# Two heads of attention side by side, and each pair's value products between the projections of the next pair

## The chip, the cores and the metric

One core of one Trainium2 chip runs the program. The time is that of the device, in microseconds, for one execution.

## The reference, cut to what matters

The input `x` has 512 tokens of width 1024. A first block (a gated convolution with a linear recurrence, then a layer that picks experts per token) changes it. A second block mixes it again, and the change lies in that one. It projects the normalised tokens to 4096 columns. Half of them feed an attention with eight heads of width 64. The other half feed four heads of a gated delta rule, a recurrence over chunks of tokens. The two outputs are gated, joined, projected back to width 1024 and added to the input.

With 512 tokens the block selection of the attention picks nothing away, so it comes down to causal attention with a slope per head:

```
logit = q @ k.T / 8 - slope * (t - s)          (for s <= t)
p     = softmax(logit)
out   = (p @ v) * silu(z)
```

## The kernel before, in words

All data of the second block is held with features on the 128 partitions and the 512 tokens along them, in float32. The projections are exact products split in three: each weight and each activation is a high part and a low part, and a projection is 3 x 8 matmuls of 128 x 128 by 512 columns (`_mm3`, lines 108 to 112, in `proj`, lines 861 to 866). The products of the attention take plain float32, and the trace shows two matmuls for each of them.

A **pair** is two heads. A projection has 128 output rows, so that head 2j lies on partitions 0 to 63 and head 2j+1 on 64 to 127. `attention(j)` (lines 1082 to 1136) works on pair j:

- Lines 1083 to 1097: four projections, for queries `aq`, keys `ak`, values and the gate `az`. The values are turned to token order by four transposes, in a bank of tag "pa" (line 1092).
- Lines 1105 to 1121, for one head: four blocks of 128 queries. Each does a product of 128 queries with the 128 to 512 keys that they may see (line 1108, contraction over the head's 64 rows), adds the slope (VectorE, line 1111), takes the maximum (1114, 1115), the exponential with its sum (ScalarE, 1116) and divides (1118, 1119).
- Lines 1122 to 1134, for the same head: four blocks of 128 keys. Each is transposed on TensorE (1126), copied out of PSUM (VectorE for odd blocks at line 1129, ScalarE for even ones at 1131) and multiplied with the values (1132), into the head's 64 rows of one bank `po`.
- Then the other head does the same two loops. At last `po` is multiplied with the gate (1135).

In PSUM, "pp" has two banks for projections, "pa" two banks, "ps" three banks for the delta rule, and "po" one bank. The logits and the transposed probabilities of the attention share the two banks of "pa".

The order of the work is woven by hand and then arranged by a list scheduler. Every routine is a generator that yields after each step. `A` is the chain of the delta heads and their recurrence; `B` is two sets of delta inputs and then `attention(0)` to `attention(3)`. `weave(A, na, B, nb)` takes `na` steps of A and spreads `nb` steps of B among them:

```
PLAN = [(18, 8), (18, 60), (12, 24)]
...
    for na, nb in PLAN:
        weave(A, na, B, nb)
    for _ in A:
        pass
    G = chain(gates_of_delta(), gated_norm())
    weave(B, 200, G, 10)
```

A pair takes 21 steps, so that the 60 and 24 of the plan hold all four pairs. `G` projects the delta rule's gates (line 1143, four projections) and transposes and gates its output (1155, 1157); it comes after A and B. The tile framework then schedules all of it by a model of time: an instruction that is ready goes ahead of one that waits, so the order on each engine in the trace is not that of the code. Each engine runs its own list in order. The weights come on SyncE's queue in the order of `ORDER` and are split by ScalarE and VectorE (lines 103, 104).

After G, lines 1195 to 1198 split the four attention outputs, lines 1200 to 1202 those of the delta rule, and lines 1223 to 1232 project back; the attention's four chunks are the first half of that sum.

Lines 912 to 919, before the attention, turn the residual to token order and write it to memory by way of five buffers of tag "lg", which the attention uses afterwards for its logits.

Of the kernel before, what the change touches and what calls it, by code (L numbers as in the profile page):

```python
# [9 lines left out]
F32 = mybir.dt.float32  # L10
# [4 lines left out]
AF = mybir.ActivationFunctionType  # L15
OP = mybir.AluOpType
AX = mybir.AxisListType
# [3 lines left out]
P = 128  # L21
T = 512
# [90 lines left out]


OHB = 2
PLAN = [(18, 8), (18, 60), (12, 24)]
ORDER = [20, 16, 24, 21, 17, 25, 22, 18, 26, 23, 19, 27, 0, 4, 8, 12, 1, 5, 9, 13, 2, 6, 10, 14, 3, 7, 11, 15, 28, 29, 30, 31]


# [653 lines left out]
def _mixer2(k, psum, pv):  # L773

    nc, tc, I = k.nc, k.tc, k.I
    ctx, c4 = ExitStack(), ExitStack()
    p4 = c4.enter_context(tc.tile_pool(name="p4", bufs=1, reuse_waits="tile"))

    def tile_(name, tag, bufs, shape=(P, T), dt=F32):
        return p4.tile(list(shape), dt, name=name, tag=tag, bufs=bufs)  # L780
# [8 lines left out]
    for b in range(3):  # L789
        tok.append([])  # L790
        for h in range(2):
            o = tile_("ptok", *(("kT", 4), ("kT", 4), ("vT", 2))[b])
# [7 lines left out]
    C = {n: cb[:, slice(*v)] for n, v in _CB.items()}  # L800
# [6 lines left out]
    pps = ctx.enter_context(tc.tile_pool(name="ps4", bufs=1, space=PSUM, reuse_waits="tile"))  # L807
# [24 lines left out]
    for dc in range(KC):  # L832
        ps = bank("pt", "pa", (P, 4, P))
        for b in range(4):
# [3 lines left out]
                                       scalar=g2[:, dc:dc + 1], in1=x, op0=OP.mult, op1=OP.add)  # L838
        nc.scalar.activation(out=hH[:, dc, :], in_=x, func=AF.Copy, scale=fp[:, dc:dc + 1])
        nc.vector.scalar_tensor_tensor(out=hL[:, dc, :], in0=x, scalar=fp[:, dc:dc + 1],  # L840
                                       in1=hH[:, dc, :].bitcast(F32), op0=OP.mult, op1=OP.subtract)
# [27 lines left out]
    ps = bank("gates", "pa")  # L869
# [5 lines left out]
    ps = bank("gatesT", "ps", (P, 4, 8))  # L875
# [36 lines left out]
    for tb in range(4):  # L912
        for hf in range(2):
            ps = bank("x2", "pa", (P, 4, P))
            for j in range(4):
                nc.tensor.transpose(ps[:, j, :], xT[hf * 4 + j][:, tb * P:(tb + 1) * P], k.ident)
            o = tile_("x3", "lg", 5)
            nc.scalar.activation(out=o, in_=ps.rearrange("p a b -> p (a b)"), func=AF.Copy, scale=r1[:, tb:tb + 1])
            nc.sync.dma_start(out=k.x3d[tb, :, hf * T:(hf + 1) * T], in_=o)
    u_all = p4.tile([P, 4, 4, P], F32, name="u_all")  # L920
# [26 lines left out]
    def delta_inputs(h, ins):  # L947

        kT = qkv(20 + h, 4 + h, "kT", 4)
        yield  # L950
        q = qkv(16 + h, h, "qT", 4)
        yield
        vT = qkv(24 + h, 8 + h, "vT", 2)
        yield
        qT.append(q)
        sq = []
        for t in (kT, q):
            o = tile_("sq", "tmp", 3)
            nc.scalar.activation(out=o, in_=t, func=AF.Square)
            sq.append([o])  # L960
        rkq = p4.tile([P, 8], F32, name="rkq", tag="rkq", bufs=2)
        rstd(rkq, _token_sums(k, pps, sq, "ps", 3), 1.0)
        rk, rq = rkq[:, 0:4], rkq[:, 4:8]
        nc.vector.tensor_scalar(out=rq, in0=rq, scalar1=128.0 ** -0.5, scalar2=None, op0=OP.mult)
        sc = p4.tile([P, 3, 4], F32, name="ksc", tag="ksc", bufs=2)
        brk, bek, kdk = sc[:, 0, :], sc[:, 1, :], sc[:, 2, :]
        nc.vector.tensor_tensor(out=brk, in0=hcols(beta, h), in1=rk, op=OP.mult)
        nc.vector.tensor_tensor(out=bek, in0=brk, in1=hcols(egc, h), op=OP.mult)
        nc.vector.tensor_tensor(out=kdk, in0=hcols(kds, h), in1=rk, op=OP.mult)
        ins.append((h, kT, q, vT, rk, rq, brk, bek, kdk))  # L970
        yield
# [107 lines left out]
            S = S2  # L1079
            yield  # L1080

    def attention(j):
        aq, ak = tile_("aq", "aq", 2), tile_("ak", "ak", 2)
        nc.vector.scalar_tensor_tensor(out=aq, in0=proj(j), scalar=0.125, in1=row2, op0=OP.mult, op1=OP.mult)
        yield
        nc.vector.tensor_tensor(out=ak, in0=proj(4 + j), in1=row2, op=OP.mult)
        yield
        vT = tile_("vT", "tmp", 3)
        nc.vector.tensor_tensor(out=vT, in0=proj(8 + j), in1=row2, op=OP.mult)
        yield  # L1090
        av = tile_("av", "av", 2, (P, 4, P))
        nc.scalar.activation(out=av, in_=tokmajor(vT, "pa"), func=AF.Copy)
        yield
        az = tile_("az", "az", 4)
        nc.vector.tensor_tensor(out=az, in0=proj(12 + j), in1=row2, op=OP.mult)
        nc.scalar.activation(out=az, in_=az, func=AF.Silu)
        yield
        po = pps.tile([P, T], F32, name="ps_ao", tag="po", bufs=1)
        for hh in range(2):
            h = 2 * j + hh  # L1100
            off = hh * 64
            rows = slice(off, off + 64)
            slope = 2.0 ** -(h + 1)
            pr = []
            for qb in range(4):
                nk = (qb + 1) * P
                ps = pps.tile([P, T], F32, name="ps_l", tag="pa", bufs=2)
                nc.tensor.matmul(out=ps[:, 0:nk], lhsT=aq[rows, qb * P:(qb + 1) * P], rhs=ak[rows, 0:nk],
                                 start=True, stop=True)
                lg = tile_("lg", "lg", 5)  # L1110
                nc.vector.scalar_tensor_tensor(out=lg[:, 0:nk], in0=C["alibi"][:, 384 - qb * P:512], scalar=slope,
                                               in1=ps[:, 0:nk], op0=OP.mult, op1=OP.add)
                mx = p4.tile([P, 2], F32, name="mx", tag="mx", bufs=6)
                nc.vector.tensor_reduce(out=mx[:, 0:1], in_=lg[:, 0:nk], axis=AX.X, op=OP.max)
                nc.vector.tensor_scalar(out=mx[:, 0:1], in0=mx[:, 0:1], scalar1=-1.0, scalar2=None, op0=OP.mult)
                nc.scalar.activation(out=lg[:, 0:nk], in_=lg[:, 0:nk], func=AF.Exp, bias=mx[:, 0:1],
                                     accum_out=mx[:, 1:2])
                nc.vector.reciprocal(out=mx[:, 1:2], in_=mx[:, 1:2])
                nc.vector.tensor_scalar(out=lg[:, 0:nk], in0=lg[:, 0:nk], scalar1=mx[:, 1:2], scalar2=None, op0=OP.mult)
                pr.append(lg)  # L1120
                yield
            for kb in range(4):
                nq = (4 - kb) * P
                ps = pps.tile([P, T], F32, name="ps_pT", tag="pa", bufs=2)
                for qb in range(kb, 4):
                    nc.tensor.transpose(ps[:, (qb - kb) * P:(qb - kb + 1) * P], pr[qb][:, kb * P:(kb + 1) * P], k.ident)
                pT = tile_("pT", "pT", 3)
                if kb % 2:
                    nc.vector.tensor_copy(out=pT[:, 0:nq], in_=ps[:, 0:nq])
                else:  # L1130
                    nc.scalar.activation(out=pT[:, 0:nq], in_=ps[:, 0:nq], func=AF.Copy)
                nc.tensor.matmul(out=po[rows, kb * P:T], lhsT=av[:, kb, off:off + 64], rhs=pT[:, 0:nq],
                                 start=kb == 0, stop=kb == 3)
                yield
        nc.vector.tensor_tensor(out=az, in0=az, in1=po, op=OP.mult)
        azs.append(az)

    zs = []

    def gates_of_delta():  # L1140
        for h in range(4):
            z = tile_("dz", ("X", "XT")[h // 2], 2)
            nc.vector.tensor_tensor(out=z, in0=proj(28 + h), in1=row2, op=OP.mult)
            nc.scalar.activation(out=z, in_=z, func=AF.Silu)
            zs.append(z)
            yield
# [3 lines left out]
    def gated_norm():  # L1150

        for h in range(4):
            ps = bank("oT", "ps", (P, 4, P))
            for tb in range(4):
                nc.tensor.transpose(ps[:, tb, :], u_all[:, tb, h, :], k.ident)
            z = zs[h]
            nc.vector.scalar_tensor_tensor(out=z, in0=flat(ps), scalar=k.col("gdn_norm"), in1=z,
                                           op0=OP.mult, op1=OP.mult)
            yd.append(z)
            yield  # L1160

    def chain(*gens):
        for g in gens:
            yield from g
# [7 lines left out]
    def weave(a, na, b, nb):  # L1172

        done = 0
        for i in range(na):
            next(a, None)
            while (done + 1) * na <= (i + 1) * nb:
                next(b, None)
                done += 1

    ins = [[], []]
# [1 line left out]
        for _ in delta_inputs(h, ins[0]):  # L1183
            pass
    A = chain(heads(ins[0]), heads(ins[1]), recurrence())
    B = chain(delta_inputs(2, ins[1]), delta_inputs(3, ins[1]), *[attention(j) for j in range(4)])
    for na, nb in PLAN:
        weave(A, na, B, nb)
    for _ in A:
        pass  # L1190
    G = chain(gates_of_delta(), gated_norm())
    weave(B, 200, G, 10)
    for _ in G:
        pass
    for az in azs:
# [181 lines left out]
```

## Time and profile before

| | us |
|---|---|
| median of 3 runs | 1889.33 |
| lowest, highest | 1887.18, 1890.7 |
| the profiled execution | 1889.39 |
| its span | 1887.6 |
| TensorE busy in it | 1798.1 |
| attention, delta rule and recurrence | from about 1555 to 1833 of the span |

The span goes from the first to the last instruction that the profile holds; the profiled execution's own time is 1.79 us longer. In a timeline, a row's length is that of its group, and groups overlap; the time from one start to the next is what an instruction costs the engine. PE is TensorE's matmuls, PEld its weight loads, DVE VectorE, ACT ScalarE and SP SyncE. "x2" counts matmuls, of which a float32 product with values or keys has two.

### The profile page before, as it was taken

Reading aid. Unit: us, or ns where it says so; the run is one execution under the profiler, and the core shown is the slowest. Engines: PE = TensorE matmul, PEld = TensorE weight load, DVE = VectorE, ACT = ScalarE, POOL = GpSimd, SP = SyncE. Lnnn points to the kernel's source line nnn. Section 1 sums busy time; section 2 is a strip of 40 time slices with the busy share of each in tenths; the row PEclk is TensorE's granted clock in tenths of the full one; section 3 lists DMA queues with packets and bytes.
Section 4 is the critical chain, followed back from the end, with each engine's and each line's share of the span. In section 5 each row is a group of like instructions: output and inputs, shape, how many; then the busy total and the mean of one; then the engine's idle time right before and its main releaser. Section 6 shows DMA issues by size and latency. Waiting matters only on the chain.

```text
span 1887.6 us, 26152 instructions
## 1 busy us (share of the span) xinstructions
PE 1798.1 (95%) x9545; PEld 1541.1 (82%) x9545; DVE 1495.1 (79%) x3045; ACT 838.9 (44%) x1186; POOL 328.1 (17%) x260
## 2 busy tenths in 40 slices
PE   6979999999996999999999999999999999999988
PEld 4756678999985999999999999988887788767778
DVE  8995589999998988888878888889945774565665
ACT  4473343456883433333333333333334753454453
POOL 0000000000000035444444444445400000000000
PEclk9989899999997999999999999999999999999999
DMA  8951323335668979999999999999952321111022
GB/s 305 314 195 56 140 82 102 118 134 201 255 236 277 291 245 380 338 344 338 330 343 344 341 336 338 342 331 343 345 182 77 103 76 56 56 45 45 12 78 90
DMA packets 153412, 404.28 MB, mean 214 GB/s; under 512 B 12097, under 2 KB 64577, under 8 KB 151746
## 3 DMA queue, kind: packets, MB, share of 16 engines
q1 hardware_dynamic: 114690, 243.20, 37.6%
q0 software_dynamic: 36864, 134.23, 19.6%
q10 hardware_dynamic: 1728, 25.17, 3.4%
q8 instruction: 75, 1.23, 0.3%
q14 instruction: 55, 0.45, 0.1%
HBM read 370.05 MB, written 32.51 MB: 213 GB/s over the span
## 4 chain that ended last, share of the span: by engine, by line
PE 78%; DVE 10%; ACT 3%; issue 1%; DMA 1%; DVEq 0%; ACTq 0%; SPq 0%
PE pv L738 9%; PE pv L741 9%; PE pv L744 9%; PE psS L112 8%; PE psS L110 8%; PE psS L111 8%; PE ps_p L110 3%; PE ps_p L111 3%; PE ps_p L112 3%; PE ps_inv L930 2%; DVE wL L104 2%; PE ps_g L652 2%; PE ps_zp L110 1%; PE ps_zp L112 1%; PE ps_zp L111 1%; DVE ohB L632 1%
## 5 line engine op out<-in xcount | busy, mean ns | idle before, releaser
L103 ACT ACTIVATE wH<-wraw 128x1024 fp32r<-128x1024 f32 x204 | 216.6, 1062 | 426.7 <-PE psS L111 268.2
L112 PE MATMUL psS<-hidH,wL 128*128 128x384 f32 x1024 | 347.1, 339 | 3.5 <-DVE wL L104 3.5
L110 PE MATMUL psS<-hidH,wH 128*128 128x384 f32 x1024 | 347.1, 339 | 3.5 <-ACT ring L546 3.5
L111 PE MATMUL psS<-hidL,wH 128*128 128x384 f32 x1024 | 346.4, 338 | 0.0
L104 DVE TENSOR_TENSOR wL<-wraw,wH 128x1024 fp32r<-128x1024 f32 x204 | 249.4, 1223 | 97.0 <-ACT wH L103 96.8
L699 POOL DMA_INDIRECT row<-uN,uidx x128 | 161.4, 1261 | 863.0 <-DVE vidx L692 681.7
L738 PE MATMUL pv<-vH,cH 128*128 128x512 f32 x768 | 223.6, 393 | 15.9 <-ACT vH L103 15.9
L744 PE MATMUL pv<-vH,cL 128*128 128x512 f32 x768 | 237.5, 390 | 0.0
L741 PE MATMUL pv<-vL,cH 128*128 128x512 f32 x768 | 237.4, 390 | 0.0
L103 ACT ACTIVATE cH<-ring 128x384 fp32r<-128x384 f32 x128 | 67.2, 525 | 326.3 <-PE pv L741 308.5
L110 PEld LDWEIGHTS psS<-hidH,wH 128*128 128x128 f32 x1024 | 193.7, 189 | 7.8 <-ACT ring L546 4.4
L112 PEld LDWEIGHTS psS<-hidH,wL 128*128 128x128 f32 x1024 | 193.3, 189 | 5.2 <-DVE wL L104 5.0
L708 POOL DMA_INDIRECT row<-vR,vidx x128 | 166.5, 1300 | 172.1 <-DVE acc L714 150.2
L111 PEld LDWEIGHTS psS<-hidL,wH 128*128 128x128 f32 x1024 | 193.4, 189 | 3.2
L738 PEld LDWEIGHTS pv<-vH,cH 128*128 128x128 f32 x768 | 143.7, 189 | 41.0 <-ACT vH L103 16.2
L104 DVE TENSOR_TENSOR vL<-vraw,vH 128x1024 fp32r<-128x1024 f32 x128 | 156.5, 1222 | 20.6 <-ACT vH L103 20.3
L744 PEld LDWEIGHTS pv<-vH,cL 128*128 128x128 f32 x768 | 144.1, 188 | 31.0
L741 PEld LDWEIGHTS pv<-vL,cH 128*128 128x128 f32 x768 | 144.1, 188 | 31.0
L714 DVE SCALAR_TENSOR_TENSOR acc<-row,act,acc 128x1024 f32<-128x1024 f32 x127 | 162.6, 1281 | 8.1 <-DMA row<-vR,vidx 7.4
L701 DVE SCALAR_TENSOR_TENSOR row<-row,h2tok 128x1024 f32<-128x1024 f32 x128 | 154.7, 1219 | 13.2 <-DMA row<-uN,uidx 12.9
L103 ACT ACTIVATE vH<-vraw 128x1024 fp32r<-128x1024 f32 x128 | 135.8, 1061 | 0.0
L104 DVE TENSOR_TENSOR cL<-ring,cH 128x384 fp32r<-128x384 f32 x128 | 71.0, 556 | 61.7 <-ACT cH L103 61.5
(416 smaller groups left out, 3041.4 us busy)
## 6 DMA issues: line engine op xcount, KB each, us to landing
wraw<-uT SPq DMA_DIRECT2D x128, 512.0 KB, 5.6
vraw<-vR SPq DMA_DIRECT2D x128, 512.0 KB, 6.3
wraw<-w_in SPq DMA_DIRECT2D x52, 512.0 KB, 3.7
wada<-wada SPq DMA_DIRECT2D x48, 512.0 KB, 4.8
gd<-st ACTq DMA_DIRECT2D x12, 2048.0 KB, 7.3
g<-gd SPq DMA_DIRECT2D x32, 768.0 KB, 9.3
wraw<-w_out SPq DMA_DIRECT2D x16, 512.0 KB, 3.5
wraw<-w_q SPq DMA_DIRECT2D x8, 512.0 KB, 3.5
```

Source lines behind the costliest of these rows:

```text
L103: copy = nc.scalar.activation(out=H, in_=src, func=AF.Copy)
L104: nc.vector.tensor_tensor(out=L, in0=src, in1=H.bitcast(F32), op=OP.subtract)
L110: nc.tensor.matmul(out=ps, lhsT=lH, rhs=rH, start=start, stop=False)
L111: nc.tensor.matmul(out=ps, lhsT=lH, rhs=rL, start=False, stop=False)
L112: nc.tensor.matmul(out=ps, lhsT=lL, rhs=rH, start=False, stop=stop)
L699: nc.gpsimd.indirect_dma_start(out=row, out_offset=None, in_=I["uN"], in_offset=bass.IndirectOffsetOnAxis(ap=uidx[:, n:n + 1], axis=0))
L701: nc.vector.scalar_tensor_tensor(out=row, in0=row, scalar=1.0, in1=h2tok, op0=OP.mult, op1=OP.mult, accum_out=act0[:, n:n + 1])
L708: nc.gpsimd.indirect_dma_start(out=row, out_offset=None, in_=k.vrows, in_offset=bass.IndirectOffsetOnAxis(ap=vidx[:, n:n + 1], axis=0))
L714: nc.vector.scalar_tensor_tensor(out=k.acc0, in0=row, scalar=act0[:, n:n + 1], in1=k.acc0, op0=OP.mult, op1=OP.add)
L738: nc.tensor.matmul(out=pv[b][h], lhsT=cH[:, bs], rhs=vH[:, h * 512:(h + 1) * 512], start=first, stop=False)
L741: nc.tensor.matmul(out=pv[b][h], lhsT=cH[:, bs], rhs=vL[:, h * 512:(h + 1) * 512], start=False, stop=False)
L744: nc.tensor.matmul(out=pv[b][h], lhsT=cL[:, bs], rhs=vH[:, h * 512:(h + 1) * 512], start=False, stop=last)
```

## The change

The two heads of a pair go through the softmax together (`softmax(j)`): for each block of queries the two products stand next to each other in the code, one on rows 0 to 63 and one on rows 64 to 127, and each takes a bank of "pa". In `values(j)` the transposes of both heads come first for a block of keys, one copy goes to ScalarE and one to VectorE, and after a yield the two products with the values stand next to each other. The values of pair j are woven with the projections of pair j+1; those of the last pair (`last`) are left over and woven with G, after A has been run to its end. The logits get eight buffers of their own widths in place of five full ones, the small sums ten buffers in place of six. The residual's copies take three buffers of tag "pT". The plan's numbers of B go from 60 and 24 to 56 and 20. The new chain has 5 + 4 x 8 + 3 x 13 = 76 steps.

```diff
-PLAN = [(18, 8), (18, 60), (12, 24)]
+PLAN = [(18, 8), (18, 56), (12, 20)]
...
-            o = tile_("x3", "lg", 5)
+            o = tile_("x3", "pT", 3)
...
-    def attention(j):
+    def projections(j, st):
...
+        st[j] = aq, ak, av, az, [[], []]
         yield
...
+    halves = [slice(0, 64), slice(64, 128)]
+
+    def softmax(j, st):
+
+        aq, ak, av, az, pr = st[j]
+        for qb in range(4):
+            nk = (qb + 1) * P
+            pss = []
+            for rows in halves:
                 ps = pps.tile([P, T], F32, name="ps_l", tag="pa", bufs=2)
                 nc.tensor.matmul(out=ps[:, 0:nk], lhsT=aq[rows, qb * P:(qb + 1) * P], rhs=ak[rows, 0:nk],
                                  start=True, stop=True)
+                pss.append(ps)
+            for hh, ps in enumerate(pss):
+                lg = tile_("lg", "lg%d" % qb, 2, (P, nk))
+                nc.vector.scalar_tensor_tensor(out=lg, in0=C["alibi"][:, 384 - qb * P:512],
+                                               scalar=2.0 ** -(2 * j + hh + 1), in1=ps[:, 0:nk],
+                                               op0=OP.mult, op1=OP.add)
+                mx = p4.tile([P, 2], F32, name="mx", tag="mx", bufs=10)
...
+                pr[hh].append(lg)
                 yield
-            for kb in range(4):
-                nq = (4 - kb) * P
+
+    def values(j, st):
+        aq, ak, av, az, pr = st[j]
+        po = pps.tile([P, T], F32, name="ps_ao", tag="po", bufs=1)
+        for kb in range(4):
+            nq = (4 - kb) * P
+            pts = []
+            for hh in range(2):
                 ps = pps.tile([P, T], F32, name="ps_pT", tag="pa", bufs=2)
                 for qb in range(kb, 4):
-                    nc.tensor.transpose(ps[:, (qb - kb) * P:(qb - kb + 1) * P], pr[qb][:, kb * P:(kb + 1) * P], k.ident)
+                    nc.tensor.transpose(ps[:, (qb - kb) * P:(qb - kb + 1) * P], pr[hh][qb][:, kb * P:(kb + 1) * P],
+                                        k.ident)
                 pT = tile_("pT", "pT", 3)
-                if kb % 2:
+                if hh:
                     nc.vector.tensor_copy(out=pT[:, 0:nq], in_=ps[:, 0:nq])
                 else:
                     nc.scalar.activation(out=pT[:, 0:nq], in_=ps[:, 0:nq], func=AF.Copy)
-                nc.tensor.matmul(out=po[rows, kb * P:T], lhsT=av[:, kb, off:off + 64], rhs=pT[:, 0:nq],
+                pts.append(pT)
+            yield
+            for rows, pT in zip(halves, pts):
+                nc.tensor.matmul(out=po[rows, kb * P:T], lhsT=av[:, kb, rows], rhs=pT[:, 0:nq],
                                  start=kb == 0, stop=kb == 3)
-                yield
+            yield
         nc.vector.tensor_tensor(out=az, in0=az, in1=po, op=OP.mult)
         azs.append(az)
 
+    def attention():
+
+        st = {}
+        yield from projections(0, st)
+        for j in range(4):
+            yield from softmax(j, st)
+            if j < 3:
+                a, b = values(j, st), projections(j + 1, st)
+                for n in range(5):
+                    next(a)
+                    yield
+                    next(b)
+                    yield
+                for _ in a:
+                    yield
+                assert next(b, None) is None
+        st["last"] = values(3, st)
+        last.append(st["last"])
...
-    B = chain(delta_inputs(2, ins[1]), delta_inputs(3, ins[1]), *[attention(j) for j in range(4)])
+    B = chain(delta_inputs(2, ins[1]), delta_inputs(3, ins[1]), attention())
     for na, nb in PLAN:
         weave(A, na, B, nb)
     for _ in A:
         pass
+    for _ in B:
+        pass
     G = chain(gates_of_delta(), gated_norm())
-    weave(B, 200, G, 10)
+    weave(last[0], 9, G, 9)
     for _ in G:
         pass
```

## Rows read from the trace of the kernel before

**Rows 1.** The page: busy time of each engine.

```profile
PE 1798.1 (95%) x9545; PEld 1541.1 (82%) x9545; DVE 1495.1 (79%) x3045; ACT 838.9 (44%) x1186; POOL 328.1 (17%) x260
```

**Rows 2.** Windows: us, busy us per engine, clock, DMA share, GB/s.

```profile
1555.00:1661.00 106.00, 105.69 (x576) 85.94 (x575) 51.72 (x95) 38.04 (x60) 0.00 (x0) 0.98 0.17 60
1661.00:1727.00 66.00, 62.27 (x320) 46.81 (x319) 44.06 (x106) 34.56 (x54) 0.00 (x0) 0.97 0.13 45
1727.00:1798.00 71.00, 68.15 (x402) 49.91 (x401) 43.40 (x105) 33.16 (x66) 0.00 (x0) 1.00 0.05 18
1798.00:1833.00 35.00, 28.28 (x191) 22.50 (x191) 24.40 (x56) 19.06 (x33) 0.00 (x0) 0.97 0.26 91
1833.00:1837.50 4.50, 4.50 (x23) 4.50 (x23) 3.42 (x6) 1.62 (x3) 0.00 (x0) 0.50 0.26 85
```

**Rows 3.** Timeline of PE, 1597 to 1608: start us, length us, instruction.

```profile
1597.33 0.48 PE L1108 MATMUL ps_l<-ak,aq 64*128 64x128 f32 x2
1597.74 1.16 PE L930 MATMUL ps_inv<-P,XT 128*128 128x128 f32 x8
...
1601.70 0.39 PE L112 MATMUL ps_p<-hidH,wL 128*128 128x512 f32 x1
1601.93 0.39 PE L110 MATMUL ps_p<-hidH,wH 128*128 128x512 f32 x1
1602.24 1.34 PE L1108 MATMUL ps_l<-ak,aq 64*128 64x256 f32 x4
1603.52 0.50 PE L111 MATMUL ps_p<-hidL,wH 128*128 128x512 f32 x1
1603.85 0.40 PE L112 MATMUL ps_p<-hidH,wL 128*128 128x512 f32 x1
...
1606.66 1.12 PE L1108 MATMUL ps_l<-ak,aq 64*128 64x512 f32 x2
1607.71 0.50 PE L112 MATMUL ps_p<-hidH,wL 128*128 128x512 f32 x1
```

**Rows 4.** Line 1108: count, duration min/median/max in ns, first and last start, forms.

```profile
L1108 PE MATMUL ps_l<-ak,aq x64: 272/481/693, 1597.3 to 1799.0; 64*128 64x128 f32 x16, 64*128 64x256 f32 x16, 64*128 64x384 f32 x16, 64*128 64x512 f32 x16
```

**Rows 5.** Timeline of PE: two products with the values, their followers.

```profile
1724.62 0.43 PE L1132 MATMUL ps_ao<-pT,av 128*64 128x128 f32 x2
1724.98 0.66 PE L937 MATMUL ps_tm<-ca,vT 128*128 128x128 f32 x4
...
1787.13 1.07 PE L1132 MATMUL ps_ao<-pT,av 128*64 128x512 f32 x2
1788.13 0.44 PE L1126 MATMUL ps_pT<-ca,lg 128*128 128x128 f32 x2
```

**Rows 6.** Timeline of PE, 1806 to 1816: the last head's values.

```profile
1806.67 0.44 PE L1126 MATMUL ps_pT<-ca,lg 128*128 128x128 f32 x2 [1.80 <-DVE lg L1119]
...
1814.37 0.86 PE L1132 MATMUL ps_ao<-pT,av 128*64 128x256 f32 x4
1815.22 1.05 PE L1061 MATMUL ps_s<-vn,ik 128*128 128x128 f32 x7
```

**Rows 7.** Waits of PE, 1555 to 1833: us in total, times, longest.

```profile
PE ps_p L110 <- DVE aq L1084: 2.5, 1, 2.5
PE ps_pT L1126 <- DVE lg L1119: 2.2, 2, 1.8
```

**Rows 8.** Timeline of DVE: the last pair's output and first split.

```profile
1815.27 0.69 DVE L1135 TENSOR_TENSOR az<-az,ps_ao 128x512 f32<-128x512 f32 x1
...
1825.65 0.69 DVE L104 TENSOR_TENSOR ya<-az,ya 128x512 fp32r<-128x512 f32 x1 [0.65 <-ACT ya L103]
```

**Rows 9.** Lines 918, 919: duration min/median/max, first and last start, landing.

```profile
L918 ACT ACTIVATE x<-ps_x,r x8: 668/671/687, 1484.0 to 1505.5; 128x512 f32<-128x512 f32 x8
...
L919 SPq DMA_DIRECT2D x3d<-x x8: 319/324/833, 1484.7 to 1506.2; - x8
...
DMA to landing us min/median/max: 2.0/2.2/4.1
```

More of the change, by code (lines that the diff above doesn't have):

```diff
@@ L1096, in attention @@
         nc.scalar.activation(out=az, in_=az, func=AF.Silu)
+        st[j] = aq, ak, av, az, [[], []]
         yield
[L1098 to L1106, printed above, removed]
+    halves = [slice(0, 64), slice(64, 128)]
[5 more added lines that the diff above has]
+            for rows in halves:
                 ps = pps.tile([P, T], F32, name="ps_l", tag="pa", bufs=2)
@@ L1109, in attention @@
                                  start=True, stop=True)
[L1110 to L1114, printed above, removed]
+                pss.append(ps)
@@ new lines, in softmax @@
+            for hh, ps in enumerate(pss):
[4 more added lines that the diff above has]
+                mx = p4.tile([P, 2], F32, name="mx", tag="mx", bufs=10)
+                nc.vector.tensor_reduce(out=mx[:, 0:1], in_=lg, axis=AX.X, op=OP.max)
@@ L1115, in attention @@
                 nc.vector.tensor_scalar(out=mx[:, 0:1], in0=mx[:, 0:1], scalar1=-1.0, scalar2=None, op0=OP.mult)
-                nc.scalar.activation(out=lg[:, 0:nk], in_=lg[:, 0:nk], func=AF.Exp, bias=mx[:, 0:1],
-                                     accum_out=mx[:, 1:2])
+                nc.scalar.activation(out=lg, in_=lg, func=AF.Exp, bias=mx[:, 0:1], accum_out=mx[:, 1:2])
                 nc.vector.reciprocal(out=mx[:, 1:2], in_=mx[:, 1:2])
-                nc.vector.tensor_scalar(out=lg[:, 0:nk], in0=lg[:, 0:nk], scalar1=mx[:, 1:2], scalar2=None, op0=OP.mult)
@@ L1120, in attention @@
-                pr.append(lg)
+                nc.vector.tensor_scalar(out=lg, in0=lg, scalar1=mx[:, 1:2], scalar2=None, op0=OP.mult)
+                pr[hh].append(lg)
                 yield
-            for kb in range(4):
-                nq = (4 - kb) * P
+    def values(j, st):
[5 more added lines that the diff above has]
+            for hh in range(2):
@@ L1131, in attention @@
                     nc.scalar.activation(out=pT[:, 0:nq], in_=ps[:, 0:nq], func=AF.Copy)
-                nc.tensor.matmul(out=po[rows, kb * P:T], lhsT=av[:, kb, off:off + 64], rhs=pT[:, 0:nq],
+                pts.append(pT)
+            yield
+            for rows, pT in zip(halves, pts):
+                nc.tensor.matmul(out=po[rows, kb * P:T], lhsT=av[:, kb, rows], rhs=pT[:, 0:nq],
                                  start=kb == 0, stop=kb == 3)
-                yield
+            yield
         nc.vector.tensor_tensor(out=az, in0=az, in1=po, op=OP.mult)
         azs.append(az)
+    def attention():
[15 more added lines that the diff above has]
+        last.append(st["last"])
+    last = []
     zs = []
```

## The prediction

> **What bounds the kernel now.** I read the page first, then windows over the stretch that the change rewrites, then TensorE's timeline inside it, then TensorE's waits. TensorE is busy for 1798.1 us of the span, 95% [rows 1], and the first four windows say the same of this stretch: from 1555 to 1833 its idle time is 0.3, 3.7, 2.9 and 6.7 us, 13.6 us in 278 [rows 2]. VectorE is busy between 49% and 70% of each window. So the stretch is bounded by the work that TensorE is given, and waits count for at most 13.6 us. A change that only moves work about can't win more than that; more must come from cheaper matmuls. The idle part is largest at the end, where no projections are left and the recurrence runs step by step.
>
> In TensorE's timeline the reader should compare starts. A logit product of 512 columns keeps the engine for 1607.71 - 1606.66 = 1.05 us, one of 128 columns for 1597.74 - 1597.33 = 0.41 [rows 3]; so a product costs 0.20 us plus 1.67 ns per column, in two matmuls [rows 4]. The row "64x256 x4" is two products in a row, of 256 and 384 columns; 1.28 us for 640 columns is 0.21 + 1.07, so the 0.20 is paid once per unbroken run, not per product. Around it, a projection matmul takes 0.23 us (1601.70 to 1601.93), but 0.31 just before the run and 0.33 just after it [rows 3]. A run of half-array products thus costs 0.20 + 0.08 + 0.10 = 0.38 us beside its columns. The products with the values cost 1.00 and 0.36 us for 512 and 128 columns [rows 5], the same 1.67 ns. Columns alone: 1280 per head, 8 heads, 17.1 us for logits and 17.1 for values.
>
> On that timeline I counted 38 runs of the lines 1108 and 1132 for their 64 products, from 1597.33 [rows 3] to 1814.37 [rows 6]; inside them the kind changes 9 times, so there are 47 runs of one kind, and 17 of the 32 possible couples stand next to each other.
>
> The sum is made against the profiled execution, 1889.39 us (span 1887.6 and 1.79 outside it); the median, 1889.33, is the same. About 0.2%, 3.8 us, is what a measurement of this kernel tells from no change.
>
> **The change part by part.**
>
> 1. *Heads next to each other on different halves of the array.* No row shows two products on different halves following each other, so what the halves gain by it is unknown. If they don't overlap: 0. If they do, matmuls still start in order: the two passes of the first product, then those of the second. The first product's second pass can then run beside the second product's first pass, and a couple takes three passes in place of four. A pass is 0.835 ns per column, 0.267 us at the mean of 320 columns. If as many couples stand together as now, 17 of 32, that gives 17 x 0.267 = 4.5 us; all 32 give 8.5. Upper bound, both passes shared and all couples together: 17.1 us. A loss is excluded only for the columns. I take 4.5, since the scheduler's present share of neighbours is the nearest thing to the future one. The Trainium skill, in "TensorEngine Tiling (Array Packing)", Theoretical Speedup, gives up to twice the speed for a dimension of 64 or less; by it the couples that stand together would save 9.1 us rather than 4.5. It says nothing of products in two passes, and no trace here shows it; it becomes a rival below.
>
> 2. *Number of runs.* Logits and values no longer meet, so runs are of one kind. All couples together: 32 runs x 0.38 = 12.2 us. None: 64 x 0.38 = 24.3. Now: 38 x 0.38 + 9 x 0.2 = 16.2. With 17 couples, 47 x 0.38 = 17.9: a loss of 1.7, which I take; the ends are a gain of 4.0 and a loss of 8.1.
>
> 3. *Values between the next projections.* The work is the same; what changes is which waits TensorE meets before the end. Its 7 us of idle before 1798 hold 2.5 for a bank of the projections, freed late by VectorE, and part of the 2.2 for the last softmax step [rows 7]. The scheduler already puts projections into the softmax's gaps [rows 3], so the weave adds little. I take a gain of 1; between a gain of 5 and a loss of 5.
>
> 4. *The last pair's values kept for the end.* From 1798 to 1833 TensorE is idle 6.7 us, and after those idle stretches the clock stands at 0.50, its 1.2 GHz level, for the 4.5 us from 1833, which costs some 2 [rows 2]. One head's transposes and values already lie there (1806.67 to 1815.22, [rows 6]); now both heads' do, about 4.7 us more work for holes of 6.7. The softmax in front must feed them: 1.8 us of the holes is a wait for its last division [rows 6, 7]. I take 4, the clock's share included; the ends are 8 and a loss, which is rival 3.
>
> 5. *Copies, buffers, plan.* Per pair VectorE copies 1280 columns in place of 1024 and ScalarE as many fewer: at 0.69 us for 512 columns [rows 8] 0.35 us of VectorE four times, in windows where it idles 30% of the time or more [rows 2]; 0. Were that cover gone, 1.4. The residual's eight copies leave over 21.5 us, 3.1 apart on average, and a write lands 2.2 us after its issue [rows 9]. With three buffers the fourth copy waits for the first write, so about 9 us lie between; 0, and at most 2 x 2.2 if the scheduler bunches them. SyncE's order of weights is unchanged, as the projections keep their order. Logit buffers are freed by the values, which end before the next softmax; 0. The plan's new numbers place 76 steps as the old ones placed 84; 0.
>
> Sum: -4.5 + 1.7 - 1 - 4 = -7.8, so 1889.4 - 7.8 = **1881.6 us**.
>
> **The rivals.**
>
> - *Rival 1, the couples never meet or don't overlap.* Both logit products need a bank of "pa" each; the two banks come free one after the other, as VectorE reads them in turn, and a projection may go between. Against it: 17 couples meet now. Then part 1 is 0, part 2 a loss of up to 8.1 (I take 4, between 1.7 and 8.1), and 5 us of idle come back: 1889.4 + 4 - 5 = 1888.4, no change. It is also the case in which "side by side" does not happen. Chance 0.22.
> - *Rival 2, all meet and the halves share the time well.* Every couple stands together (4.0 us from part 2), and the columns save between one pass (8.5) and both (17.1); with 5 to 7 us of idle gone: 1889.4 - 8.5 - 4.0 - 6 = 1870.9, and down to 1862 with both passes. For it: both copies of a block go to two engines and end together. By "TensorEngine Tiling (Array Packing)" of the Trainium skill, Theoretical Speedup, this would be the case to expect. Chance 0.2.
> - *Rival 3, slower: the last pair's values miss the recurrence.* They stand behind all of A in the code. Now the last gated output is ready at 1816 and split at 1825.7 [rows 8], ten us to spare. If the values go behind the recurrence's matmuls, from about 1826, two heads need some 9 us as one needs 8.5 now [rows 6], plus two splits and the product of 0.69: ready at about 1837. The projection back waits in its fourth chunk, and the recurrence's holes stay. TensorE would idle some 6 us more while both pairs of banks are held, and with the 1.7 of part 2 and nothing from part 4: 1889.4 + 6 + 1.7 - 1 = 1896. It decides when the last output comes after about 1829, when the three earlier chunks are used up. Against it: the scheduler has pulled projections far ahead of their place, and will pull these as soon as they are ready. Chance 0.13.
>
> **How the numbers follow.** The forecast has a chance of 0.45, with a range of its own of 1876 to 1885.5. Rivals 1, 2 and 3 have 0.22, 0.2 and 0.13. The predicted time is the forecast's. The range of 8 in 10 takes in rival 1 with its dearer runs and most of rival 2: 1867 to 1893; what is left out is rival 3 and the best end of rival 2. Faster: the forecast and rival 2, less a little for the forecast's upper end, 0.64. Same: rival 1, 0.22. Slower: rival 3 and a little, 0.14.
>
> **What would show it.** Right: in TensorE's timeline, rows of line-1108 and line-1132 successors with four matmuls of one width, whose time to the next instruction is 0.20 us plus three passes (1.48 us at 512 columns, against 1.05 for one product); some 47 runs; idle from the softmax to the projection back under 4 us; the clock at 1.0 as the projection back begins. Wrong: four full passes in such a row (no overlap), more than 55 runs, or the last gated output less than 4 us ahead of the first projection back. A time above 1893 would mean that a wait has opened which I don't see.

## The result, and the profile after

| | before | after |
|---|---|---|
| median, us | 1888.26 (4 runs, 1883.38 to 1890.7) | 1868.40 (4 runs, 1866.72 to 1868.99) |
| ratio | | 0.9891, 95% interval 0.9877 to 0.9905 |
| span of the profiled execution, us | 1887.6 | 1867.0 |
| first logit product to the end of the span, us | 290.3 | 268.0 |

The change saves 20 us, 1.1%; 1881.6 was predicted, with 1867 to 1893 as the range; the median lies 1.4 us inside its lower end. The instructions in front of the first logit product stand in the same order in both kernels, so what the change does lies behind it: 22.3 us of one profiled execution. The page of the changed kernel has the span and the busy time to set beside [rows 1]; its windows answer to [rows 2], with the third and fourth cut where the recurrence begins here (us, busy us of each engine with instructions, clock, DMA share, GB/s).

```profile
span 1867.0 us, 26156 instructions
...
PE 1784.5 (96%) x9545; PEld 1533.4 (82%) x9545; DVE 1493.7 (80%) x3045; ACT 833.5 (45%) x1183; POOL 328.0 (18%) x260
```

```profile
1555.00:1661.00 106.00, 105.69 (x583) 84.93 (x582) 55.20 (x108) 38.47 (x64) 0.00 (x0) 0.98 0.16 55
1661.00:1727.00 66.00, 65.68 (x380) 52.42 (x379) 50.08 (x117) 36.80 (x61) 0.00 (x0) 1.00 0.19 63
1727.00:1790.00 63.00, 60.57 (x382) 44.77 (x379) 42.50 (x102) 32.20 (x62) 0.00 (x0) 1.00 0.11 39
1790.00:1814.40 24.40, 19.56 (x153) 17.27 (x151) 16.17 (x36) 11.30 (x22) 0.00 (x0) 1.00 0.16 56
1814.40:1867.00 52.60, 44.91 (x373) 44.70 (x372) 28.00 (x48) 16.71 (x45) 0.00 (x0) 0.96 0.25 91
```

TensorE does the same 9545 matmuls in 13.6 us less busy time, and from 1661 to 1727 it is idle 0.3 us where it was idle 3.7. In the stretch of the recurrence (1790 to 1814.4) it is still idle 4.8 us.

Where the 22.3 us went, summed over TensorE's timeline from the first logit product on, from each start to the next, with idle time apart:

| us of TensorE | before | after | difference |
|---|---|---|---|
| logit products | 22.01 | 13.76 | -8.25 |
| value products | 20.61 | 18.65 | -1.96 |
| projections to queries, keys, values, gates | 86.43 | 84.17 | -2.26 |
| projection back | 48.93 | 46.90 | -2.03 |
| all else | 90.90 | 88.97 | -1.93 |
| idle | 13.30 | 7.59 | -5.70 |
| after the last matmul | 8.12 | 7.98 | -0.14 |
| sum | 290.30 | 268.03 | -22.27 |

Not all of the rows without idle time are work. In the kernel before, the clock stands at 0.50, its 1.2 GHz level, in two stretches, one that begins as the wait of 2.5 us for a projection's bank ends, and one at the projection back; in the changed kernel it is at 1.00 from 1597 to 1863. Two windows of before and one of after, then TensorE's timeline of before around the first stretch:

```profile
1697.60:1701.00 3.40, 3.04 (x7) 2.46 (x8) 3.40 (x9) 1.20 (x4) 0.00 (x0) 0.50 0.00 0
1830.70:1837.50 6.80, 6.31 (x29) 5.92 (x30) 5.14 (x9) 2.53 (x4) 0.00 (x0) 0.50 0.17 56
```

```profile
1597.00:1863.20 266.20, 254.72 (x1629) 207.86 (x1628) 174.38 (x388) 122.61 (x235) 0.00 (x0) 1.00 0.16 55
```

```profile
1697.96 0.79 PE L110 MATMUL ps_p<-hidH,wH 128*128 128x512 f32 x1 [2.48 <-DVE aq L1084]
...
1701.07 0.39 PE L111 MATMUL ps_p<-hidL,wH 128*128 128x512 f32 x1
1701.30 0.39 PE L112 MATMUL ps_p<-hidH,wL 128*128 128x512 f32 x1
```

The seven projection matmuls from 1697.96 to 1701.07 take 3.1 us, where seven at 0.23 take 1.6. So 1.5 us of the projections' 2.26 are the clock. So are the projection back's 2.0, and 0.5 of "all else" (the gated norm's transposes, 2.9 us before and 2.4 after): 4.0 us of the 22.3 in all.

The largest part is in the logits. These are three couples of the changed kernel's timeline of TensorE, logits of 256 and of 512 columns and values of 512, each with its successor; then two value products of the last pair that belong together and are parted (start, length, instruction).

```profile
1657.30 0.70 PE L1111 MATMUL ps_l<-ak,aq 64*128 64x256 f32 x4
1657.93 0.50 PE L112 MATMUL ps_p<-hidH,wL 128*128 128x512 f32 x1
...
1670.52 1.13 PE L1111 MATMUL ps_l<-ak,aq 64*128 64x512 f32 x4
1671.58 0.50 PE L111 MATMUL ps_p<-hidL,wH 128*128 128x512 f32 x1
...
1687.59 1.08 PE L1147 MATMUL ps_ao<-pT,av 128*64 128x512 f32 x4 [0.32 <-ACT pT L1143]
1688.60 0.33 PE L1137 MATMUL ps_pT<-ca,lg 128*128 128x128 f32 x1
...
1775.41 1.07 PE L1147 MATMUL ps_ao<-pT,av 128*64 128x512 f32 x2
1776.42 0.55 PE L1137 MATMUL ps_pT<-ca,lg 128*128 128x128 f32 x3
1776.89 1.07 PE L1147 MATMUL ps_ao<-pT,av 128*64 128x512 f32 x2
1777.90 0.55 PE L1137 MATMUL ps_pT<-ca,lg 128*128 128x128 f32 x3
```

"x4" is two products of two passes each. The two logit products of 512 columns keep the engine for 1671.58 - 1670.52 = 1.06 us; one alone took 1.05 [rows 3]. Those of 256 take 0.63, the values 1.01. So a couple costs what one product costs. The last four rows show what happens otherwise: 1.01 us for one value product of 512 columns, transposes, and the same again.

TensorE's waits after the change, from 1595 to the end (us in total, times, longest):

```profile
PE ps_s L1061 <- DVE vn L1056: 2.3, 3, 0.8
PE ps_oT L1190 <- DVE u_all L1077: 1.5, 1, 1.5
PE ps_tm L937 <- DVE X L1013: 1.2, 1, 1.2
...
PE ps_ao L1147 <- ACT pT L1143: 0.3, 1, 0.3
```

The same two waits before, from 1594 to the end:

```profile
PE ps_oT L1155 <- DVE u_all L1077: 1.5, 1, 1.5
PE ps_s L1061 <- DVE vn L1056: 1.3, 2, 0.8
```

The two waits of [rows 7], 2.5 us for a projection's bank and 2.2 for the last softmax step, are gone. The gated norm's wait (`ps_oT`) is as it was. The recurrence's (`ps_s`) comes three times where it came twice: before, the last head's values stood in front of one of its steps [rows 6]. The last pair's output and the first split of it, on VectorE, answer to [rows 8]:

```profile
1788.27 0.68 DVE L1150 TENSOR_TENSOR az<-az,ps_ao 128x512 f32<-128x512 f32 x1
...
1807.46 0.69 DVE L104 TENSOR_TENSOR ya<-az,ya 128x512 fp32r<-128x512 f32 x1 [0.65 <-ACT ya L103]
```

### The profile page after: what moved, and what is told of

Read it like the earlier page. It is cut to its first block, busy times and chain, and to the rows that moved or that the text cites. A ratio compares the mean times of both kernels' runs of the same rounds, so it can differ in the third digit from the quotient of the medians.

```text
span 1867.0 us, 26156 instructions
## 1 busy us (share of the span) xinstructions
PE 1784.5 (96%) x9545; PEld 1533.4 (82%) x9545; DVE 1493.7 (80%) x3045; ACT 833.5 (45%) x1183; POOL 328.0 (18%) x260
## 4 chain that ended last, share of the span: by engine, by line
PE 79%; DVE 10%; ACT 2%; issue 1%; DMA 1%; DVEq 0%; ACTq 0%; SPq 0%
PE pv L738 9%; PE pv L741 9%; PE pv L744 9%; PE psS L112 8%; PE psS L111 8%; PE psS L110 8%; PE ps_p L111 3%; PE ps_p L110 3%; PE ps_p L112 3%; PE ps_inv L930 2%; DVE wL L104 2%; PE ps_g L652 2%; PE ps_zp L110 1%; PE ps_zp L112 1%; PE ps_zp L111 1%; DVE ohB L632 1%
## 5 line engine op out<-in xcount | busy, mean ns | idle before, releaser
L738 PE MATMUL pv<-vH,cH 128*128 128x512 f32 x768 | 223.7, 393 | 15.8 <-ACT vH L103 15.8
L738 PEld LDWEIGHTS pv<-vH,cH 128*128 128x128 f32 x768 | 143.7, 189 | 40.9 <-ACT vH L103 16.1
L701 DVE SCALAR_TENSOR_TENSOR row<-row,h2tok 128x1024 f32<-128x1024 f32 x128 | 154.7, 1219 | 18.7 <-DMA row<-uN,uidx 18.7
```

The source lines that it names most:

```text
L701: nc.vector.scalar_tensor_tensor(out=row, in0=row, scalar=1.0, in1=h2tok, op0=OP.mult, op1=OP.mult, accum_out=act0[:, n:n + 1])
L738: nc.tensor.matmul(out=pv[b][h], lhsT=cH[:, bs], rhs=vH[:, h * 512:(h + 1) * 512], start=first, stop=False)
```

## The experiments

Each kernel has four to six timed executions, and its ratio is to the kernel before, timed beside it: 1888.1 us for e1, e2, e3 and e5, 1886.0 for the changed kernel again, e4, e6 and e8, and 1886.6 for e9. Profiled executions of one and the same order in front of the first logit product reach it anywhere from 1593.6 to 1599.0 us, so the table also gives the time from there to the end, in which two executions of the changed kernel agree to 0.02 us. The other kernels have one such figure each.

| kernel | median, us | ratio, 95% interval | first logit to end | logits | values | idle |
|---|---|---|---|---|---|---|
| changed kernel | 1868.40 | 0.9891, 0.9877 to 0.9905 | 268.03 | 13.8 | 18.7 | 7.6 |
| e1 both heads on one half | 1873.69 | 0.9921, 0.9907 to 0.9935 | 274.3 | 20.8 | 18.7 | 5.9 |
| e2 side by side only | 1874.18 | 0.9916, 0.9902 to 0.993 | 274.0 | 15.1 | 20.4 | 8.2 |
| e3 weave only | 1878.70 | 0.9944, 0.9931 to 0.9958 | 281.9 | 21.1 | 20.7 | 8.3 |
| e5 products one block later | 1869.87 | 0.9899, 0.9884 to 0.9914 | 273.9 | 14.3 | 19.3 | 8.3 |
| changed kernel again | 1865.01 | 0.9885, 0.9866 to 0.9906 | 268.04 | 13.8 | 18.6 | 7.6 |
| e4 nothing kept for the end | 1864.02 | 0.9886, 0.9865 to 0.9906 | 268.0 | 13.8 | 18.7 | 7.6 |
| e6 value couples held | 1863.03 | 0.9877, 0.9857 to 0.9896 | 264.3 | 15.1 | 11.9 | 8.3 |
| e8 all couples held | 1862.48 | 0.9872, 0.9853 to 0.9891 | 266.0 | 16.1 | 11.0 | 8.5 |
| e9 whole array | 1866.49 | 0.9888, 0.9872 to 0.9904 | 270.1 | 14.5 | 16.8 | 9.4 |

**e1: the same order, without the overlap** (both products are computed from the first head's rows, so the second head's result is left out)

```diff
-            for rows in halves:
+            for rows in (halves[0], halves[0]):
                 ps = pps.tile([P, T], F32, name="ps_l", tag="pa", bufs=2)
```

> Both heads' logits are computed from the queries and keys on rows 0 to 63 (the second head's own logits are left out and the first head's stand in their place). The order of all instructions on every engine is that of the changed kernel. Theory 1 (the two halves of the array share the time): a run of two products takes 0.20 us plus the columns of both, where the changed kernel takes those of one; 14 of the 16 couples do so there, so TensorE's logits take some 7.5 us more (13.8 to about 21.5 us) and the time is about 1876 us. Theory 2 (the gain comes from the new order, by fewer waits and fewer runs): the order is the same, so the time stays at 1868.4 us and the runs keep their length.

Measured: 1873.69 us, 5.3 more than the changed kernel, with intervals of the ratios that do not meet. TensorE's timeline of the two logit couples that were shown above:

```profile
1657.39 1.13 PE L1111 MATMUL ps_l<-ak,aq 64*128 64x256 f32 x4
1658.44 0.50 PE L112 MATMUL ps_p<-hidH,wL 128*128 128x512 f32 x1
...
1671.63 1.98 PE L1111 MATMUL ps_l<-ak,aq 64*128 64x512 f32 x4
1673.54 0.50 PE L111 MATMUL ps_p<-hidL,wH 128*128 128x512 f32 x1
```

The couple of 512 columns takes 1.91 us where it took 1.06, that of 256 takes 1.05 instead of 0.63, in the same place of the same list. The logits take 20.75 us in place of 13.76. Of these 7.0 us the engine gets 1.7 back, as longer products fill waits (idle 5.9), and the projection back is 1.0 slower; from the first logit the difference is 6.3. Theory 1 holds, and this is the cleanest evidence of it: nothing but the half of the array differs.

**e2: heads side by side, without the weave**

```diff
             yield from softmax(j, st)
+            yield from values(j, st)
             if j < 3:
-                a, b = values(j, st), projections(j + 1, st)
...
+                yield from projections(j + 1, st)
```

> Heads side by side as in the changed kernel, but each pair's values follow its softmax at once and the next projections follow the values; nothing is kept for the end; the plan's numbers are 60 and 24 as before. Theory 1 (halves share the time, the weave adds the rest): logits about 14 us of TensorE, idle between 1597 us and the end back from 7.6 to about 13 us, time about 1874 us. Theory 2 (the weave makes the gain): time near 1888 us.

Measured: 1874.18 us, the number of theory 1, but not for its reason. Idle time came back by 0.6 us only, to 8.2. What came back is work of TensorE, 5.3 us: 48 runs of half-array products in place of 39, 12 logit couples together instead of 14, and one value couple instead of 6, with one more across widths. The weave's worth lies in what it puts next to each other more than in the waits that it hides.

**e3: the weave, without heads side by side**

```diff
-        for qb in range(4):
...
-            for hh, ps in enumerate(pss):
+        for hh, rows in enumerate(halves):
+            for qb in range(4):
...
-                pts.append(pT)
-            yield
-            for rows, pT in zip(halves, pts):
```

> The weave of values with the next projections and the last pair kept for the end, but one head after the other in softmax and values, as before. Theory 1 (halves share the time, the weave adds the rest): logits 22 us and values 20 us of TensorE as before, idle 8 us, no slow clock at the projection back: about 1878 us. Theory 2 (the weave makes the gain): about 1869 us. If the weave is worth nothing alone: 1888 us.

Measured: 1878.70 us. Logits (21.1 us beside 22.0) and values (20.7 beside 20.6) are near those of before, and idle is 8.3 us, both as theory 1 has it. Its other sign failed: the clock does fall, to 0.50 from 1820.1 to 1826.9, and the projection back takes 48.9 us as before. Two rows of TensorE's waits, from 1594 to the end, show that the weave removes the old waits and brings others: the second one does not appear in the lists of the kernels before and after.

```profile
PE ps_s L1061 <- DVE vn L1056: 2.3, 3, 0.8
PE ps_inv L930 <- ACT dz L1172: 2.2, 1, 2.2
```

So the weave alone gives 9 us against the kernel before, side by side alone 14, both 20. Each alone brings idle time from 13.3 to some 8 us, so their gains overlap.

**e5: the products written one block later**

```diff
-            yield
-            for rows, pT in zip(halves, pts):
-                nc.tensor.matmul(...)
+            ready.append((kb, pts))
+            yield
+            if kb:
+                products()
+            if kb == 3:
+                products()
...
-                pT = tile_("pT", "pT", 3)
+                pT = tile_("pT", "pT", 4)
```

> As the changed kernel, but a block's two value products are written one block later, behind the transposes and copies of the next block, with four buffers for the copies. In the changed kernel 6 of the 16 value couples stand together and take the time of one; the other 10 are parted by transposes. Theory 1 (couples on different column halves share the time whenever they stand together): with all 16 together the 10 would save 6.0 us of columns and 3.8 us of run overhead, time down to about 1859 us; with half of them about 1863. Theory 2 (the transposes between are not the cause, the couples stay parted or the longer lag makes TensorE wait): 1868 us or more.

Measured: 1869.87 us, no gain. Only three value couples of one width stand together, with two more across widths, and there are 41 runs; the transposes, now behind runs more often, take 11.5 us in place of 9.4. The profiled execution was the slowest of the four, and 1.5 us of the 5.8 that it loses from the first logit lie in the projection back (48.4 us in place of 46.9). It is theory 2 in its first form: the lag does not bring the couples together. Why the scheduler parts them even so is open.

**The changed kernel again**

> The changed kernel itself, as the measure for the three kernels beside it. Every theory: 1868.4 us, within 3.

Measured: 1865.01 us, 0.4 outside what was expected, and 268.04 us from the first logit, as in the first profile. Two medians of one kernel, taken apart, differ by 3.4 us (those of the kernel before by 2.3), so e4, e6 and e8, timed together with this run, are set beside it. For e9, timed apart, the ratio to the kernel before is the one to compare.

**e4: nothing kept for the end**

```diff
-        st["last"] = values(3, st)
-        last.append(st["last"])
+        yield from values(3, st)
...
-    weave(last[0], 9, G, 9)
```

> As the changed kernel, but the last pair's values follow its softmax within the chain B (plan 56 and 28) instead of being kept until the recurrence has been woven to its end. Theory 1 (the scheduler moves work that is ready to where TensorE is free, so its place in the code matters little): the order differs in few instructions, the time is 1868 us, within 2. Theory 2 (what was kept back fills the recurrence's holes, as the prediction's part 4 had it): some 4 us of idle come back, 1872 us.

Measured: 1864.02 us beside 1865.01 for the changed kernel, and 268.0 us from the first logit in both. Theory 1 holds, and more than it said: TensorE, VectorE and ScalarE run the very order of the changed kernel, without a difference. In the changed kernel the last pair's products lie at 1775 to 1788, before the recurrence's steps, although the code has them behind it.

**e6: the first product held behind the second**

```diff
-            for rows, pT in zip(halves, pts):
-                nc.tensor.matmul(out=po[rows, kb * P:T], lhsT=av[:, kb, rows], rhs=pT[:, 0:nq],
-                                 start=kb == 0, stop=kb == 3)
+            for hh in (1, 0):
+                with ExitStack() if hh else tc.issue_after(late.ins):
+                    late = nc.tensor.matmul(out=po[halves[hh], kb * P:T], lhsT=av[:, kb, halves[hh]],
+                                            rhs=pts[hh][:, 0:nq], start=kb == 0, stop=kb == 3)
```

The edge makes the product that is ready first wait for the one whose copy ends later, so that nothing comes between them.

> As the changed kernel, but of a block's two value products the one whose copy comes later is written first and the other is held behind it, so that all 16 couples stand together (6 before), in 31 runs in place of 39. Four more logit couples are shifted by one block. Theory 1 (a couple on two column halves takes the time of one product): ten couples save 6.0 us of columns, eight runs 3 us, and the shifted logits give back some 2: values from 18.7 to about 10 us of TensorE, time about 1861 us. Theory 2 (holding makes TensorE wait for the later copy): values shrink, idle grows by as much, 1868 us.

Measured: 1863.03 us. The values take 11.9 us in place of 18.7, idle rises by 0.7, the projection back by 1.0, and the logits by 1.3: in three of the four pairs a product now overlaps with one of another width and leaves single ones over, so 13 logit couples are together where 14 were. There are 31 runs, and in all 16 value couples the products stand together. One of the 16, at 1683.85, still takes 1.81 us: its second product starts 0.8 us after the first, and what held it is open. The 512-column group of the value products in the changed kernel (instructions | busy us, mean ns | idle before), and in e6 that couple and one of the last pair, each with its successor, and the same group:

```profile
L1147 PE MATMUL ps_ao<-pT,av 128*64 128x512 f32 x16 | 7.5, 618 | 0.3 <-ACT pT L1143 0.3
```

```profile
1683.85 1.88 PE L1148 MATMUL ps_ao<-pT,av 128*64 128x512 f32 x4
1685.66 0.44 PE L1137 MATMUL ps_pT<-ca,lg 128*128 128x128 f32 x2
...
1768.37 1.08 PE L1148 MATMUL ps_ao<-pT,av 128*64 128x512 f32 x4
1769.38 0.44 PE L1137 MATMUL ps_pT<-ca,lg 128*128 128x128 f32 x2
...
L1148 PE MATMUL ps_ao<-pT,av 128*64 128x512 f32 x16 | 5.1, 618 | 0.0
```

The two products that were parted above, 1775.41 and 1776.89, now stand together, 1.01 us for both, and the group's busy time goes from 7.5 to 5.1 us. Theory 1 holds for column halves as e1 does for row halves. From the first logit, e6 is 3.7 us ahead of the changed kernel; the medians, 1863.03 and 1865.01, differ by 2.0 with ranges that overlap (1861.83 to 1864.18, 1862.28 to 1867.78). It beats the kernel before clearly, and the changed one by about the scatter.

**e8: the logits held as well**

```diff
-            for rows in halves:
-                ps = pps.tile([P, T], F32, name="ps_l", tag="pa", bufs=2)
...
+            for hh in (1, 0):
+                with ExitStack() if hh else tc.issue_after(late.ins):
+                    late = nc.tensor.matmul(out=pss[hh][:, 0:nk], lhsT=aq[halves[hh], qb * P:(qb + 1) * P],
+                                            rhs=ak[halves[hh], 0:nk], start=True, stop=True)
```

> As e6_hold_values, and the logits held in the same way, so that the couples of one width stand together except three that other work parts, in 33 runs. Theory 1: logits at or below 13.8 us of TensorE, values 10, time 1860 to 1862 us. Theory 2 (waiting for the second bank costs more than the couple saves): above e6_hold_values by 2 us or more.

Measured: 1862.48 us, within the scatter of e6; from the first logit 266.0, which is 1.7 more. That need not be the holding: e8's clock is at 0.50 from 1730.0 to 1733.4, where e6's is not. The logits rose to 16.1 us, against at most 13.8 expected by theory 1. Five logit couples are parted now, where in e6 shifted ones overlap all the same. Holding the logits gains nothing.

**e9: the whole array, and no halves**

```diff
+        for hh in range(2):
+            nc.gpsimd.memset(aq[hh][halves[1 - hh], :], 0.0)
+            nc.gpsimd.memset(av[hh][:, :, halves[1 - hh]], 0.0)
...
-                nc.tensor.matmul(out=ps[:, 0:nk], lhsT=aq[rows, qb * P:(qb + 1) * P], rhs=ak[rows, 0:nk],
+                nc.tensor.matmul(out=ps[:, 0:nk], lhsT=aq[hh][:, qb * P:(qb + 1) * P], rhs=ak[:, 0:nk],
...
-                nc.tensor.matmul(out=po[rows, kb * P:T], lhsT=av[:, kb, rows], rhs=pT[:, 0:nq],
-                                 start=kb == 0, stop=kb == 3)
+                nc.tensor.matmul(out=po[:, kb * P:T], lhsT=av[hh][:, kb, :], rhs=pT[:, 0:nq],
+                                 start=kb == 0 and hh == 0, stop=kb == 3 and hh == 1)
```

> As the changed kernel, but no product uses half of the array: each head has its own queries with zeros on the other head's rows, and its own values with zeros in the other head's columns, so that all 64 products take all 128 rows and columns and both heads' values add up in the same bank. Nothing can overlap, and the array never changes its shape; GpSimd writes the zeros, VectorE and ScalarE each have one more instruction per pair and use. Theory 1 (a run of half-array products costs 0.38 us beside its columns because the shape changes): logits and values take 17.1 us each plus little, the neighbours' 0.18 us per run goes too, 34 to 36 us in all against 13.8 + 18.7 + 7 in the changed kernel; time 1863 to 1866 us. Theory 2 (the 0.38 us is the price of any float32 product that follows another kind of matmul): logits 20.7, values 20.6 us, neighbours as before, time about 1876 us.

Measured: 1866.49 us. A value product of 512 columns on the whole array, with its neighbours, on TensorE's timeline:

```profile
1626.07 0.40 PE L110 MATMUL ps_p<-hidH,wH 128*128 128x512 f32 x1
1626.30 0.40 PE L111 MATMUL ps_p<-hidL,wH 128*128 128x512 f32 x1
1626.54 1.02 PE L1155 MATMUL ps_ao<-pT,av 128*128 128x512 f32 x2
1627.39 0.49 PE L1145 MATMUL ps_pT<-ca,lg 128*128 128x128 f32 x3
```

It keeps the engine for 1627.39 - 1626.54 = 0.85 us, 512 columns at 1.67 ns and nothing else, and the projection before it for 0.24, as in the middle of a projection. So the 0.38 us of a run is the price of the change of shape, as theory 1 has it. Logits and values take 31.3 us together, about as much as the changed kernel's 32.4 with its overlaps; the end of a product before a projection is partly booked on that, but with the projections it is the same picture, 117.3 us against 116.6. The time is 0.5 us above what was expected, as idle is 1.8 us and the projection back 1.5 us above the changed kernel's.

## Why the prediction was right, and where it was not

The bound was read rightly: TensorE's own work, with at most 13.6 us of idle. Of the gain, 5.7 us are idle time and 16.4 TensorE's instructions, 4.0 of these by the clock. The direction and the range held, the range by 1.4 us, which is less than the 3.4 between two medians of one kernel, and so with some luck. The sum was 7.8 us and the profile shows 22.3; the time is nearer to rival 2 (1870.9) than to the forecast.

*Part 1, overlap: the term that was mis-sized.* It had three passes for a couple, since matmuls start in order, and 17 couples: 4.5 us. The passes of the two products go in step: the second product adds 0.01 us to the first, both on row halves and on column halves. 14 logit couples saved 7.0 us (e1), and the six value couples, 1536 columns at 1.67 ns, 2.6. That is 9.6 us with 20 couples. The signature was to be 1.48 us for a couple of 512 columns; it is 1.06. Rival 2 named the full overlap, but not this case: it had all 32 couples together, and 4.0 us from fewer runs that did not come, so its time is near by other terms. By "TensorEngine Tiling (Array Packing)" of the Trainium skill, Theoretical Speedup, it is up to twice the speed, and the trace agrees: 1.06 us for two products against 1.91 on one half.

*Part 2, runs.* A loss of 1.7 was taken from 47 runs at 0.38 us, all of one kind since logits and values no longer meet. They do meet: there are 39 runs, with 5 changes of kind inside, which makes 39 x 0.38 + 5 x 0.2 = 15.8 against 16.2: no loss. That the price is one of shape is what e9 shows. Part of it lies in the neighbours, and so in the 0.8 us of the projections and the 1.5 of "all else" that are not the clock. Overlap (9.6), idle time (5.7), clock (4.0) and runs (0.4) leave some 2.6 of the 22.3 us, which no run divides further.

*Part 3, the weave.* A gain of 1 was taken, with 5 as its end. Waits outside the recurrence and the gated norm fell from 9.3 us to 2.5, by 6.8. With the wait of 2.5 us went the slow clock behind it, 1.5 us, which no part had, although the window of that wait shows a clock of 0.97 [rows 2]. But e2, without the weave, is idle 8.2 us only, so most of this comes with the pairing too. What the weave itself is worth, 6 us from the first logit (e2 against the changed kernel), is mostly couples and runs, and no part of the prediction had that.

*Part 4, the last pair for the end: wrong.* The recurrence's holes were to be filled, for 2 of the 4 us. They grew: the waits of the recurrence came to 2.1 us before and come to 3.0 now, those of the gated norm to 1.9 and 2.1. The values were not there to fill them, as the scheduler had pulled them ahead (e4); before, one head's values had filled one hole. What left the stretch is the softmax's wait of 1.8. The other 2 us of this part, the clock, did come, but not for the reason given, filled holes; see below.

*Part 5, copies, buffers, plan.* Nothing in the profile speaks against its zeros: the order in front of the first logit is the same.

Of the signs named, the clock at 1.00 came, and so did the idle time under 4 us, 3.0 from the last pair's values to the projection back's first matmul. The couple of 1.48 us and the 47 runs did not.

Rival 3 needed the last output late; it is ready at 1788.95, some 19 us before the projection back starts at 1808.07. Rival 1 is refuted by e1 and by the couples themselves.

## What to carry to other kernels

Two float32 products on different halves of the array cost what one does if they follow each other with nothing between and start together; whether they do is decided by what each waits for. Holding the product that is ready first behind the other brought the value products together (e6), but gained nothing for the logits (e8), so count the couples in the order of instructions and read their lengths in the trace. Every change of shape has a price too, here 0.38 us for a run against none on the whole array with zeros; by these figures, as an estimate, a couple at 0.38 + 1.67 ns per column beats two whole-array products at 3.34 ns per column only above 0.38 / 0.00167 = 230 columns. A wait can cost more than its length, here 2.5 us and 1.5 more by the clock behind it. Work that is moved in the source for a scheduler that sorts by readiness may not move at all.

## What was not expected of the hardware

**The clock at the projection back.** Windows of equal length from where the projection back begins, in the kernel before, the changed one and e6 (us, busy us per engine, clock):

```profile
1826.20:1850.20 24.00, 22.06 (x154) 20.84 (x153) 17.68 (x27) 8.89 (x20) 0.00 (x0) 0.86 0.19 60
```

```profile
1808.00:1832.00 24.00, 21.85 (x173) 20.55 (x172) 18.02 (x28) 9.97 (x21) 0.00 (x0) 1.00 0.19 67
```

```profile
1800.00:1824.00 24.00, 21.86 (x164) 20.80 (x163) 17.56 (x27) 9.23 (x21) 0.00 (x0) 0.93 0.20 64
```

All three hold the same idle 1.9 to 2.2 us, but the granted clock is 0.86, 1.00 and 0.93 on the mean, and the projection back takes 48.9, 46.9 and 47.9 us. So the same wait costs 2, 0 or 1 us by the clock's fall to its 1.2 GHz level or its absence. It is no chance of one execution: three of the changed kernel's order (itself, again, and e4) take 46.9 us, and so does e2; e1, in that order with longer logits, takes 47.9. What decides it no run shows.

**The scatter in front.** With one order of TensorE's, VectorE's and ScalarE's instructions up to the first logit product, ten profiled executions (that of before, and nine of the changed kernel and the experiments) reach it between 1593.6 and 1599.0 us, and e9, with two more instructions on VectorE, lies between. Some of it arises early: the first matmul into psS already starts between 293.3 and 298.5. The rest of the way takes between 1297.6 and 1301.7. This is as large as the differences between the experiments. The time from a common instruction to the end leaves it out, and three executions of one order agree in it to 0.04 us; but it is one execution's, and a change of the clock moves it by up to 2 us.
